# Splitting the first MLP into two blocks of two tiles, and replacing the two small ScalarE steps of the threshold search by one VectorE operation, in a hybrid-attention block

## The chip, the cores and the metric

The kernel runs on one core of a Trainium2 chip. The metric is device time in microseconds (us), the median of several runs; the parts are read from one execution taken by the hardware profiler.

## The reference

One transformer block in float32 on `x` of 1024 tokens by 1024 features. Three residual parts follow one another, each behind an RMS norm:

```
x = x + hybrid_mixer(rms_norm(x))      # DSA top-k attention, and NSA: compressed + window + selected
x = x + memory_xattn(rms_norm(x), mem) # 4 heads over 256 memory tokens
x = x + square(relu(rms_norm(x) @ w_ff_in)) @ w_ff_out   # 1024 -> 4096 -> 1024
...
idx_score = einsum(relu(q_i @ k_i), w_i)        # per query, over all earlier keys
_, sel = top_k(idx_score, 256)                  # DSA attends to those 256 keys alone
```

For this length the NSA branch selects every admissible block, so only DSA needs a search: for each query, the 256th largest index score.

## The kernel before

**Tiles and stages.** The 1024 tokens are eight tiles of 128, numbered 0 to 7. A head stage projects tiles 0 to 3. Then *attention* goes through tiles 0 to 7 (`attend`); beside it a second stream, the *fill*, does work that needs no attention yet or no longer: the projection of tiles 4 to 7, the memory's keys and values (`memory`), then for finished tiles `between` (output projection, norm, memory attention) and `mlp`. Behind attention come what is left of the fill, `between` for tiles 6 and 7, and the last MLP for tiles 4 to 7.

**Order.** `together` draws from two generators. Attention yields its estimated PE time; the fill is drawn while its own sum is at most `pace` times attention's. A tuple `(need, pace)` from the fill holds it until attention has passed tile `need` and sets a new pace; the paces are `PACES`. Behind attention, `merge` draws from the rest of the fill and from `between(d2, 6, 2, ...)` in proportion to `REST` and 45. The order of drawing is a priority; a scheduler of the framework then sets a fixed order of instructions for each engine, and each engine runs its list in order.

**The fill before.** `memory`, then `between(dn, 0, 2)`, `between(dn, 2, 2)`, `mlp(dn, 0, 4)` and `between(dn, 4, 2)`; the two numbers are the first tile and how many.

**MLP and weights.** A float32 product is made of three single-pass products of rounded parts (`whi`, `wlo` for weights; `xh`, `xl` or a pair of `h` tiles for data). `load_w` brings 256 KB into a `wraw` buffer, ScalarE rounds it into `whi` (L244), and the difference goes into `wlo` (L249), on GpSimd where the entry of `PLAN_MAIN` or `PLAN_TAIL` is "ag" and on VectorE where it is "av". Up-projection: stationary weights, moving data `[128, nt*128]`, 24 matmuls for each of 32 column groups. Down-projection: stationary data, 512 moving weight columns. The residual is added at L891. Where one pass is not needed in parts (`load_whole`, L265) a full float32 product is used; those weights share the buffers of `whi` and `wlo`.

**Rings.** `RINGS` gives the buffers of each tag in a pool. `dn` is the fill's pool, `d2` the last MLP's. PSUM has two banks of tag D and one of M for the fill, and S, PT, PV for attention; `d2` takes S and PT.

**The search.** `index_mask` for tile t+1 runs beside attention of tile t, for t+1 from 2 to 7: scores, then a binary search over 16 high and 16 low bits. Each step is three ScalarE operations, each waiting for the one before: count the scores over the threshold (`Sign` with `accum_out`, L636), compare the count (L637), move the threshold (L638).

Of the kernel before, what the change touches and what calls it, by code (L numbers as in the profile page):

```python
# [9 lines left out]
F32 = mybir.dt.float32  # L10
# [25 lines left out]
RINGS = {  # L36
    "p1": {"x4": 5, "st": 2, "relu": 4, "wraw": 4, "whi": 6, "wlo": 6, "c8": 4, "c4": 2, "kraw": 5, "pc": 2},
    "p2": {"x4": 3, "st": 1, "relu": 2, "whi": 4, "wlo": 4, "c8": 3, "c4": 1, "kraw": 4, "pc": 2},
    "dn": {"b4": 4, "h": 8, "relu": 2, "wraw": 2, "whi": 4, "wlo": 4},
    "d2": {"b4": 4, "h": 8, "relu": 2, "wraw": 3, "whi": 6, "wlo": 6},  # L40
}
PSUMS = {"p1": {"D": 4, "M": 3, "C": 1}, "main": {"S": 2, "PT": 2, "PV": 1, "D": 2, "M": 1}}
TAGS = {"p1": ("D", "M", "C"), "p2": ("D", "M", "D"), "dn": ("D", "M"), "d2": ("S", "PT")}
PLAN_HEAD = ("ag", "av")
PLAN_MAIN = ("ag",)
PLAN_TAIL = ("ag", "av", "ag")

SLC, WIN, DSA, IDX = 0, 2, 4, 5
# [28 lines left out]
        "c_cmask": np.ascontiguousarray(cm.transpose(1, 0, 2)),  # L77
    }
TC_ARGS = {"schedule_with_timeline_sim": True}
PACES = (1.35, 1.35, 1.35, 1.75, 1.75)  # L80
REST = 70.0


def drain(gen):
# [21 lines left out]
def merge(a, b):  # L106
    drain(beside(*a, *b))


def together(att, fill, projected):  # L110


    da = df = lead = 0.0
    tile_, need, part, pace = -1, -2, 0, PACES[0]
    la = lf = True
    while la:
        held = part > len(projected)
        if lead is None and need < tile_:
            lead = df - da * pace
        if lf and need < tile_ and (held or df <= lead + da * pace):  # L120
            w = next(fill, None)
            lf = w is not None
            if isinstance(w, tuple):
                need, pace = w
                lead = None
            else:
                df += w or 0.0
        else:
            assert not held
            x = next(att, None)  # L130
            la = x is not None
            if la and x[1] is None:
                part += 1
            elif la:
                tile_ = x[0]
                da += x[1]


# [28 lines left out]
def build(nc, tc, I, C, out):  # L167
# [92 lines left out]

    def load_whole(pool, shape, *srcs):
        wholes["i"] += 1
        raw = ring(pool, ("whi", "wlo")[wholes["i"] % 2], shape)
        for dst, src in srcs:
            nc.sync.dma_start(dst(raw), src)  # L265
        return [raw]
# [58 lines left out]
                consume(ci, t, pt)  # L325
                yield nk * (5 - len(xs)) * w / 2400.0

    def xT(pool, nt, whole=False):

        parts = [pool.tile([P, DM // P, nt * P], F32 if whole else F32R, tag="x" + n, name="x" + n)  # L330
                 for n in ("h" if whole else "hl")]
        return (parts, [lambda t, k, x=x: x[:, k, t * P:(t + 1) * P] for x in parts],
                lambda t: [x[:, :, t * P:(t + 1) * P] for x in parts])

# [257 lines left out]
    def index_mask(aw, st, t):  # L592
        Wd = (t + 1) * P
        acc = small(aw, "isc", L, bufs=1)
        for hg in range(2):
            qh, ql = q_prep(aw, t, 2, hg)
            for h in range(4):
                for c, n in chunks_of(t + 1):
                    sp = pst("S", [P, n * P])
                    mv = st["K"][:, IDX, c * P:(c + n) * P]  # L600
                    mm(sp, qh[:, h, :], mv, True, False)
                    mm(sp, ql[:, h, :], mv, False, True)
                    r = small(aw, "ir", 512)
# [12 lines left out]
        sgn = mask.bitcast(I16)  # L616
        hi, lo = small(aw, "tkh", L, U16, 1)[:, :Wd], small(aw, "tkl", L, U16, 1)[:, :Wd]
        v.tensor_scalar(sgn, bits[:, :, 1], 0.0, -1.0, op0=ALU.is_lt, op1=ALU.mult)
        v.scalar_tensor_tensor(hi.bitcast(I16), sgn, -32768, bits[:, :, 1], op0=ALU.bitwise_or, op1=ALU.bitwise_xor)
        v.tensor_tensor(lo.bitcast(I16), bits[:, :, 0], sgn, op=ALU.bitwise_xor)  # L620


        cnt, low = small(aw, "tkc", 1), small(aw, "tkf", 1)
        over, step, need = small(aw, "tko", 1), small(aw, "tks", 1), small(aw, "tkg", 2)
        th = small(aw, "tkt", 2)
        v.memset(need[:, 0:1], Wd - 2 * TOPK + 1.0)
        v.memset(th, 0.5 - 32768.0)
        for half, src in enumerate((hi, lo)):
            c, nd = th[:, half:half + 1], need[:, half:half + 1]
            if half == 1:  # L630
                v.tensor_scalar(low, th[:, 0:1], -1.0, None, op0=ALU.mult)
                v.tensor_scalar(mask, hi, low, None, op0=ALU.is_gt, op1=ALU.add, accum_out=cnt)
                v.tensor_scalar(nd, cnt, 2.0, Wd - 2 * TOPK + 1.0, op0=ALU.mult, op1=ALU.add)
                v.scalar_tensor_tensor(lo, hi, low, lo, op0=ALU.is_equal, op1=ALU.mult)
            for b in range(15, -1, -1):
                s.activation(mask, src, AF.Sign, bias=c, accum_out=over)  # L636
                s.activation(step, over, AF.Sign, bias=nd)  # L637
                s.activation(c, step, AF.Identity, scale=-0.5 * (1 << b), bias=c)  # L638
# [254 lines left out]

    def between(pool, t0, nt, x2s, keep):

        o_of = []
        for t in range(nt):
            o = ring(pool, "b4", [P, 8, P])
            for c in range(8):
                nc.sync.dma_start(o[:, c, :], oT_dr[t0 + t][c])  # L900
            o_of.append(o)
        x2 = [ring(pool, "b4", [P, DM]) for t in range(nt)]
        for t in range(nt):
            nc.sync.dma_start(x2[t], I["x"][0, (t0 + t) * P:(t0 + t + 1) * P, :])
        add_to = residual_add(x2)
        four = [[(c * 256, 256)] for c in range(4)]
        yield from gemm(pool, [lambda t, k: o_of[t][:, k, :]], 8, nt, W["w_out"], four, add_to)
        _, xf, xt_of = xT(pool, nt, True)

        gb2 = gain2(pool, W["norm2_g"])  # L910
        for t in range(nt):
# [82 lines left out]
    def mlp(pool, t0, nt, x2s):  # L994
# [13 lines left out]
        for f4 in range(8):  # L1008
# [24 lines left out]
            for c in range(2):  # L1033
# [4 lines left out]
                for t in range(nt):  # L1038
# [11 lines left out]
                                          x2[t][:, c * 512:(c + 1) * 512])  # L1050
                    yield 2.6

    def pe_stack():
        pe = p1.tile([P, 2, 32], F32, tag="pe", name="pe")
        pe2 = ring(p1, "relu", [P, 2, 2, 64])
# [18 lines left out]
        "dm": {},  # L1074
        "ix": set(),
    }
    for kv in range(2):
        v.memset(st["cT"][kv], 0.0)
    pe = pe_stack()
# [7 lines left out]
    dn_pool = tc.tile_pool(name="dn", bufs=1, reuse_waits="tile")  # L1087
    aw = aw_pool.__enter__()
    projected = []

    def fill():
        for part in range(1, len(PARTS)):
# [3 lines left out]
        dn = dn_pool.__enter__()  # L1096
        yield from memory(dn)
        yield 1, PACES[1]
        yield from between(dn, 0, 2, {}, False)
        yield 3, PACES[2]  # L1100
        x2s = {}
        yield from between(dn, 2, 2, x2s, True)
        yield 3, PACES[3]
        yield from mlp(dn, 0, 4, x2s)
        yield 5, PACES[4]
        yield from between(dn, 4, 2, {}, False)

    rest = fill()
    together(attend(aw, st), rest, projected)
    aw_pool.__exit__(None, None, None)  # L1110
    at_pool.__exit__(None, None, None)
    d2_pool = tc.tile_pool(name="d2", bufs=1, side="right", reuse_waits="tile")
# [1 line left out]
    d2 = d2_pool.__enter__()  # L1114
    x2s = {}
    rest = (w for w in rest if not isinstance(w, tuple))
    merge((rest, REST), (between(d2, 6, 2, x2s, True), 45.0))
    dn_pool.__exit__(None, None, None)
    drain(mlp(d2, 4, 4, x2s))
    d2_pool.__exit__(None, None, None)  # L1120
    ctx.close()

# [20 lines left out]
```

## Time and profile before

| | us |
|---|---|
| median of 3 runs | 1808.53 (1806.28 to 1810.84) |
| the profiled execution, its own time | 1807.76 |
| its span in the trace | 1806.0 |
| TensorE busy, as recorded | 1700.2 |
| ScalarE busy | 1061.9 |
| VectorE busy | 927.8 |
| GpSimd busy | 887.4 |

PE is TensorE's matmul row, PEld its weight loads, DVE is VectorE, ACT ScalarE, POOL GpSimd, SP the queue that issues DMAs. A matmul's record is longer than the time for which it holds the array, because matmuls overlap; the distance between the starts of two matmuls in a dense stretch tells what one costs. A row of a group reads: line, engine, operation, output<-inputs, shape, count | busy us, mean ns of one | idle time of the engine just before, and what ended it. A row of the table by stages gives the stretch, its length, and for each engine busy us and, in brackets, instructions; then the granted TensorE clock, the DMA share and GB/s.

### The profile page before, as it was taken

The numbers are of one execution on the slowest core, as the hardware profiler recorded it, in microseconds if no ns is written. First come the engines' busy times: TensorE is split into PE (matmuls) and PEld (weight loads), VectorE is DVE, ScalarE is ACT, GpSimd is POOL, SyncE is SP. The second block draws the span as 40 slices with busy tenths as digits, with TensorE's granted clock in tenths as the row PEclk, the third lists the DMA queues.
The fourth block names the chain that finished last, engine by engine and source line by source line (L and its number), as shares of the span: only waits on it lengthen the run. The fifth ranks groups of instructions, "written<-read, shape, count | busy, mean of one in ns | idle before, by whom it ended". The sixth has DMA issues, their size and how long they took to land. (4 is left out here: it accounts for less than half of the span.)

```text
span 1806.0 us, 27690 instructions
## 1 busy us (share of the span) xinstructions
PE 1700.2 (94%) x9134; PEld 1447.8 (80%) x9134; DVE 927.8 (51%) x2343; ACT 1061.9 (59%) x2655; POOL 887.4 (49%) x1015
## 2 busy tenths in 40 slices
PE   5987999899989999999998999999999799999998
PEld 5986888688878777788886888888888687787887
DVE  4545757665874776375754555646524322222221
ACT  4445669797688579855896558994513333333332
POOL 2356647363541355568575667662111144545444
PEclk9998999999999999999999999999999799999999
DMA  6235221366336211212122212226384122222222
GB/s 193 73 121 155 70 68 58 114 196 175 102 109 196 87 59 42 75 65 80 59 75 75 62 65 78 65 74 194 98 284 151 47 87 89 97 91 96 94 95 93
DMA packets 171887, 185.38 MB, mean 103 GB/s; under 512 B 26464, under 2 KB 140896, under 8 KB 171744
## 3 DMA queue, kind: packets, MB, share of 16 engines
q1 hardware_dynamic: 163808, 173.13, 30.3%
q0 software_dynamic: 7936, 10.49, 2.2%
q8 instruction: 72, 1.18, 0.3%
q14 instruction: 71, 0.58, 0.1%
HBM read 162.59 MB, written 20.97 MB: 102 GB/s over the span
## 5 line engine op out<-in xcount | busy, mean ns | idle before, releaser
L249 POOL TENSOR_TENSOR wlo<-wraw,whi 128x512 fp32r<-128x512 f32 (+1 forms) x231 | 310.6, 1351 | 280.9 <-ACT whi L244 252.9
L244 ACT ACTIVATE whi<-wraw 128x512 fp32r<-128x512 f32 (+2 forms) x289 | 181.0, 628 | 250.8 <-PE psS L218 156.8
L218 PE MATMUL psD<-whi,xh 128*128 128x256 f32 (+1 forms) x704 | 191.1, 352 | 4.4 <-ACT whi L244 3.4
L218 PE MATMUL psD<-wlo,xh 128*128 128x256 f32 (+1 forms) x704 | 190.3, 352 | 1.6 <-DMA wlo<-in_w_in_dram 1.0
L236 DVE TENSOR_TENSOR pl<-psPT,ph 128x512 fp32r<-128x512 f32 (+1 forms) x232 | 142.1, 621 | 78.9 <-ACT ph L235 76.3
L218 PE MATMUL psD<-whi,h 128*128 128x512 f32 x512 | 174.3, 403 | 3.7 <-ACT whi L244 1.6
L218 PE MATMUL psS<-whi,h 128*128 128x512 f32 x512 | 162.4, 392 | 5.4 <-DVE b L891 5.4
L680 ACT ACTIVATE S<-S,mn 128x128 f32<-128x128 f32 (+7 forms) x192 | 142.7, 744 | 40.5 <-DVE mn L678 39.0
L685 POOL TENSOR_SCALAR S<-S,sums,gi 128x640 f32<-128x640 f32 (+7 forms) x128 | 107.8, 853 | 114.1 <-DVE sums L683 103.5
L235 ACT ACTIVATE ph<-psPT 128x512 fp32r<-128x512 f32 (+1 forms) x232 | 122.9, 540 | 61.5 <-PE psPT L695 57.1
L249 DVE TENSOR_TENSOR wlo<-wraw,whi 128x512 fp32r<-128x512 f32 (+1 forms) x58 | 56.3, 971 | 170.3 <-ACT whi L244 170.1
L218 PEld LDWEIGHTS psD<-wlo,xh 128*128 128x128 f32 x704 | 132.4, 193 | 13.6 <-DMA wlo<-in_w_in_dram 1.4
L218 PEld LDWEIGHTS psD<-whi,xh 128*128 128x128 f32 x704 | 130.0, 193 | 14.2 <-ACT whi L244 3.8
L695 PE MATMUL psPT<-c_ident,S 128*128 128x128 f32 x816 | 131.8, 277 | 3.9 <-POOL S L685 2.6
L891 DVE TENSOR_TENSOR b<-psS,b 128x512 f32<-128x512 f32 (+1 forms) x80 | 49.9, 636 | 138.5 <-PE psS L218 138.5
L218 PE MATMUL psS<-K,qh 128*128 128x384 f32 (+3 forms) x288 | 112.4, 394 | 8.9 <-DVE mn L678 3.9
L218 PEld LDWEIGHTS psS<-whi,h 128*128 128x128 f32 x512 | 96.0, 188 | 30.4 <-DVE b L891 10.1
L218 PEld LDWEIGHTS psD<-whi,h 128*128 128x128 f32 x512 | 95.5, 189 | 25.8 <-ACT whi L244 2.0
L695 PEld LDWEIGHTS psPT<-c_ident,S 128*128 128x128 f32 x816 | 97.6, 142 | 14.1 <-POOL S L685 4.5
L218 PE MATMUL psD<-wlo,h 128*128 128x512 f32 x256 | 102.6, 404 | 1.1 <-POOL wlo L249 1.1
L218 PE MATMUL psD<-xh,wlo 128*128 128x512 f32 x256 | 101.5, 398 | 0.0
L891 DVE TENSOR_TENSOR b<-psD,b 128x512 f32<-128x512 f32 (+1 forms) x112 | 63.2, 573 | 74.0 <-PE psD L218 66.9
(289 smaller groups left out, 4546.2 us busy)
## 6 DMA issues: line engine op xcount, KB each, us to landing
wraw<-in_w_ff_in_dram SPq DMA_DIRECT2D x128, 256.0 KB, 2.7
wraw<-in_w_ff_out_dram SPq DMA_DIRECT2D x128, 256.0 KB, 2.6
whi<-in_w_out_dram SPq DMA_DIRECT2D x32, 256.0 KB, 3.8
wlo<-in_w_out_dram SPq DMA_DIRECT2D x32, 256.0 KB, 4.3
wraw<-in_w_in_dram SPq DMA_DIRECT2D x24, 256.0 KB, 3.4
q<-st SPq DMA_DIRECT2D x12, 512.0 KB, 2.6
qin<-q SPq DMA_DIRECT2D x44, 128.0 KB, 2.3
x<-in_x_dram SPq DMA_DIRECT2D x8, 512.0 KB, 5.5
```

The source lines that it names most:

```text
L218: te.matmul(o, a, b, start=start, stop=stop)
L235: s.activation(hi, src, AF.Copy)
L236: v.tensor_tensor(lo, src, hi, op=ALU.subtract)
L244: s.activation(hi, raw, AF.Copy)
L249: (v if l == "v" else g).tensor_tensor(lo, raw, hi, op=ALU.subtract)
L680: s.activation(S, S, AF.Exp, bias=low, scale=-1.0, accum_out=sums[:, hh:hh + 1])
L685: g.tensor_scalar(Ss[hh], Ss[hh], sums[:, hh:hh + 1], 1.0 if gate is None else gate[:, hh:hh + 1], op0=ALU.mult, op1=ALU.mult)
L695: te.transpose(p2[:, j, hh, :], S[:, (c + j) * P:(c + j + 1) * P], ident)
L891: v.tensor_tensor(dst, pt, dst, op=ALU.add)
```

## The change

Five edits belong together.

1. `mlp(dn, 0, 4)` becomes `mlp2` twice, for tiles 0 and 1 and for tiles 2 and 3. A block's up-projection moves 256 columns instead of 512, and each block loads and splits all MLP weights, so that they are loaded twice. `mlp2` has rings of its own (`hs`, `mr`).
2. The fill's order: `between(0, 2)`, then `two_streams`, which draws the MLP blocks as the main stream and, beside it, `between` for one tile at a time: tile 2, tile 3 (before the second block may start), then tiles 4 and 5 beside the second block. A single tile may start once attention has left it behind.
3. `load_whole` in pool `dn` has a ring of its own, `wb`, of two buffers, instead of the eight of `whi` and `wlo`.
4. In the search, the compare and the move become one VectorE `scalar_tensor_tensor` with accumulator: of three columns [-2^b, threshold, 2^b/2] those whose count exceeds the need are summed; two columns always do.
5. `PLAN_MAIN` sends a third of the `wlo` subtractions to VectorE, the last two paces go from 1.75 to 1.5, and behind attention `between(6, 2)` is followed by the first steps (the norms) of the last MLP, both beside the rest of the fill.

The diff, cut; `mlp2` is otherwise `mlp` with two tiles.

```diff
-    "dn": {"b4": 4, "h": 8, "relu": 2, "wraw": 2, "whi": 4, "wlo": 4},
+    "dn": {"b4": 4, "h": 7, "hs": 8, "mr": 2, "relu": 2, "wb": 2, "wraw": 2, "whi": 4, "wlo": 4},
-PLAN_MAIN = ("ag",)
+PLAN_MAIN = ("ag", "av", "ag")
-PACES = (1.35, 1.35, 1.35, 1.75, 1.75)
-REST = 70.0
+PACES = (1.35, 1.35, 1.35, 1.5, 1.5)
+SIDE = 0.9
+REST = 110.0
...
-        raw = ring(pool, ("whi", "wlo")[wholes["i"] % 2], shape)
+        raw = ring(pool, "wb" if "wb" in RINGS.get(pool.name, ()) else ("whi", "wlo")[wholes["i"] % 2], shape)
...
-        over, step, need = small(aw, "tko", 1), small(aw, "tks", 1), small(aw, "tkg", 2)
+        over, tks, need = st["tko"], st["tks"], small(aw, "tkg", 2)
         th = small(aw, "tkt", 2)
-        v.memset(need[:, 0:1], Wd - 2 * TOPK + 1.0)
-        v.memset(th, 0.5 - 32768.0)
+        v.memset(need[:, 0:1], 2.0 * TOPK - 1.0 - Wd)
         for half, src in enumerate((hi, lo)):
-            c, nd = th[:, half:half + 1], need[:, half:half + 1]
+            nd = need[:, half:half + 1]
             if half == 1:
                 v.tensor_scalar(low, th[:, 0:1], -1.0, None, op0=ALU.mult)
                 v.tensor_scalar(mask, hi, low, None, op0=ALU.is_gt, op1=ALU.add, accum_out=cnt)
-                v.tensor_scalar(nd, cnt, 2.0, Wd - 2 * TOPK + 1.0, op0=ALU.mult, op1=ALU.add)
+                v.tensor_scalar(nd, cnt, -2.0, 2.0 * TOPK - 1.0 - Wd, op0=ALU.mult, op1=ALU.add)
                 v.scalar_tensor_tensor(lo, hi, low, lo, op0=ALU.is_equal, op1=ALU.mult)
             for b in range(15, -1, -1):
-                s.activation(mask, src, AF.Sign, bias=c, accum_out=over)
-                s.activation(step, over, AF.Sign, bias=nd)
-                s.activation(c, step, AF.Identity, scale=-0.5 * (1 << b), bias=c)
+                i = 15 - b
+                s.activation(mask, src, AF.Sign, bias=tks[:, i, 1:2], accum_out=over[:, 0:1])
+                v.scalar_tensor_tensor(small(aw, "tkj", 3), over, nd, tks[:, i, :], op0=ALU.is_gt, op1=ALU.mult,
+                                       accum_out=tks[:, i + 1, 1:2] if b else th[:, half:half + 1])
                 yield 0.1
...
-        o_of = []
+        one = "b" if nt == 1 else "h"
+        (o,), xf, _ = xT(pool, nt, True, one)
         for t in range(nt):
-            o = ring(pool, "b4", [P, 8, P])
             for c in range(8):
-                nc.sync.dma_start(o[:, c, :], oT_dr[t0 + t][c])
-            o_of.append(o)
+                nc.sync.dma_start(o[:, c, t * P:(t + 1) * P], oT_dr[t0 + t][c])
         x2 = [ring(pool, "b4", [P, DM]) for t in range(nt)]
         for t in range(nt):
             nc.sync.dma_start(x2[t], I["x"][0, (t0 + t) * P:(t0 + t + 1) * P, :])
         add_to = residual_add(x2)
         four = [[(c * 256, 256)] for c in range(4)]
-        yield from gemm(pool, [lambda t, k: o_of[t][:, k, :]], 8, nt, W["w_out"], four, add_to)
-        _, xf, xt_of = xT(pool, nt, True)
+        yield from gemm(pool, xf, 8, nt, W["w_out"], four, add_to)
+        _, xf, xt_of = xT(pool, nt, True, one)
...
+    def mlp2(pool, t0, x2s):
...
+                c0 = (f4 * 4 + f2 * 2) * P
+                for k0 in range(0, 8, KG):
+                    hi, lo = load_w(pool, [P, KG, 256], (lambda r: r, W["w_ff_in"][k0 * P:(k0 + KG) * P, c0:c0 + 256]
+                                                         .rearrange("(k p) n -> p k n", p=P)))
...
+                    pt = pst(TAGS[pool.name][0], [P, 256])
+                    fs = slice(f * P, (f + 1) * P)
+                    for k in range(8):
+                        wh, wl = gr[k]
+                        mm(pt, wh[:, fs], xh[:, k, :], k == 0, False)
+                        mm(pt, wl[:, fs], xh[:, k, :], False, False)
+                        mm(pt, wh[:, fs], xl[:, k, :], False, k == 7)
+                    hh, hl = ring(pool, "hs", [P, 256], F32R), ring(pool, "hs", [P, 256], F32R)
+                    r = ring(pool, "mr", [P, 256])
+                    s.activation(r, pt, AF.Relu)
+                    s.activation(r, r, AF.Square)
+                    g.tensor_scalar(hh, r, 1.0, 1.0, op0=ALU.mult, op1=ALU.mult)
+                    g.tensor_tensor(hl, r, hh, op=ALU.subtract)
+                    hs.append((hh, hl))
+                    yield 2.6
...
+    st["tks"] = at.tile([P, 16, 3], F32, tag="tks", name="tks")
+    st["tko"] = at.tile([P, 3], F32, tag="tko", name="tko")
+    v.memset(st["tko"], BIG)
+    v.memset(st["tks"][:, 0, 1:2], 0.5 - 32768.0)
+    for i in range(16):
+        v.memset(st["tks"][:, i, 0:1], -1.0 * (1 << (15 - i)))
+        v.memset(st["tks"][:, i, 2:3], 0.5 * (1 << (15 - i)))
...
-        yield from between(dn, 0, 2, {}, False)
-        yield 3, PACES[2]
         x2s = {}
-        yield from between(dn, 2, 2, x2s, True)
-        yield 3, PACES[3]
-        yield from mlp(dn, 0, 4, x2s)
-        yield 5, PACES[4]
-        yield from between(dn, 4, 2, {}, False)
+        yield from between(dn, 0, 2, x2s, True)
+        yield seen["tile"] - 1, PACES[2]
+        yield from two_streams(dn, x2s)
+
+    def two_streams(dn, x2s):
+
+
+        main, mains = mlp2(dn, 0, x2s), 1
+        side, t = None, 2
+        dm = ds = 0.0
+        while main or side or mains < 2 or t < 6:
+            if side is None and t < 6 and seen["tile"] > t and (t < 4 or mains == 2):
+                side, ds = between(dn, t, 1, x2s, t < 4), dm
+                if t == 4:
+                    yield seen["tile"] - 1, PACES[3]
+            if main is None and mains == 1 and side is None and t >= 4:
+                main, mains = mlp2(dn, 2, x2s), 2
+            if side and (main is None or ds <= dm):
+                w = next(side, None)
+                ds += (w or 0.0) / SIDE
+                if w is None:
+                    side, t = None, t + 1
+            elif main:
+                w = next(main, None)
+                dm += w or 0.0
+                if w is None:
+                    main = None
+            elif t < 6:
+                w = t, PACES[3]
+            if w is not None:
+                yield w
 
     rest = fill()
-    together(attend(aw, st), rest, projected)
+    together(attend(aw, st), rest, projected, seen)
+    seen["tile"] = NT
     aw_pool.__exit__(None, None, None)
     at_pool.__exit__(None, None, None)
     d2_pool = tc.tile_pool(name="d2", bufs=1, side="right", reuse_waits="tile")
@@ -1114,9 +1203,10 @@
     d2 = d2_pool.__enter__()
     x2s = {}
     rest = (w for w in rest if not isinstance(w, tuple))
-    merge((rest, REST), (between(d2, 6, 2, x2s, True), 45.0))
+    last = mlp(d2, 4, 4, x2s)
+    merge((rest, REST), (chain(between(d2, 6, 2, x2s, True), take(last, 4.0)), 62.0))
     dn_pool.__exit__(None, None, None)
-    drain(mlp(d2, 4, 4, x2s))
+    drain(last)
     d2_pool.__exit__(None, None, None)
```

More of the change, by code (lines that the diff above doesn't have):

```diff
@@ L107, in merge, with together @@
     drain(beside(*a, *b))
-def together(att, fill, projected):
+def together(att, fill, projected, seen):
     da = df = lead = 0.0
@@ L134, in together @@
             elif la:
-                tile_ = x[0]
+                tile_ = seen["tile"] = x[0]
                 da += x[1]
@@ L326, in gemm, with xT @@
                 yield nk * (5 - len(xs)) * w / 2400.0
-    def xT(pool, nt, whole=False):
+    def xT(pool, nt, whole=False, one="h"):
         parts = [pool.tile([P, DM // P, nt * P], F32 if whole else F32R, tag="x" + n, name="x" + n)
-                 for n in ("h" if whole else "hl")]
+                 for n in (one if whole else "hl")]
         return (parts, [lambda t, k, x=x: x[:, k, t * P:(t + 1) * P] for x in parts],
@@ L1051, in mlp @@
                     yield 2.6
+    def mlp2(pool, t0, x2s):
+        x2 = [x2s[t0], x2s[t0 + 1]]
+        (xh, xl), _, xt_of = xT(pool, 2)
+        gb3 = gain2(pool, W["norm3_g"])
+        for t in range(2):
+            norm_T2(pool, x2[t], gb3, xt_of(t))
+            yield 1.0
+        for f4 in range(8):
+            hs = []
+            for f2 in range(2):
+                gr = []
+                c0 = (f4 * 4 + f2 * 2) * P
+                for k0 in range(0, 8, KG):
+                    hi, lo = load_w(pool, [P, KG, 256], (lambda r: r, W["w_ff_in"][k0 * P:(k0 + KG) * P, c0:c0 + 256]
+                                                         .rearrange("(k p) n -> p k n", p=P)))
+                    gr += [(hi[:, k, :], lo[:, k, :]) for k in range(KG)]
+                for f in range(2):
+                    pt = pst(TAGS[pool.name][0], [P, 256])
[13 more added lines that the diff above has]
+                    yield 2.6
+            for c in range(2):
+                cs = slice(c * 512, (c + 1) * 512)
+                gr = []
+                for k in range(4):
+                    r0 = (f4 * 4 + k) * P
+                    gr.append(load_w(pool, [P, 512], (lambda r: r, W["w_ff_out"][r0:r0 + P, cs])))
+                for t in range(2):
+                    pt = pst(TAGS[pool.name][0], [P, 512])
+                    us = slice(t * P, (t + 1) * P)
+                    for f in range(4):
+                        hh, hl = hs[f]
+                        wh, wl = gr[f]
+                        mm(pt, hh[:, us], wh, f == 0, False)
+                        mm(pt, hh[:, us], wl, False, False)
+                        mm(pt, hl[:, us], wh, False, f == 3)
+                    v.tensor_tensor(x2[t][:, cs], pt, x2[t][:, cs], op=ALU.add)
+                    if f4 == 7:
+                        nc.sync.dma_start(out[0, (t0 + t) * P:(t0 + t + 1) * P, cs], x2[t][:, cs])
+                    yield 2.6
@@ L1089, in build @@
     projected = []
+    seen = {"tile": -1}
     def fill():
```

## The prediction

> **What bounds the kernel now.** I read the page first, then the table by stages, then single stretches of the timeline, to learn what a matmul costs where nothing holds it.
>
> ```profile
> PE 1700.2 (94%) x9134; PEld 1447.8 (80%) x9134; DVE 927.8 (51%) x2343; ACT 1061.9 (59%) x2655; POOL 887.4 (49%) x1015
> ```
>
> TensorE looks 94% busy, but its records overlap. The timeline shows the true price by the distance of starts:
>
> ```profile
> 100.11 0.28 PE L218 MATMUL psD<-whi,xh 128*128 128x256 f32 x1
> ...
> 100.45 0.28 PE L218 MATMUL psD<-whi,xh 128*128 128x256 f32 x1
> ...
> 103.74 0.82 PE L474 MATMUL psM<-c_ident,x 128*128 128x128 f32 x6
> 104.31 0.37 PE L218 MATMUL psD<-whi,xl 128*128 128x256 f32 x1
> ```
>
> ```profile
> 1417.15 1.03 PE L218 MATMUL psS<-wlo,xh 128*128 128x256 f32 x4
> 1418.02 1.03 PE L218 MATMUL psS<-whi,xh 128*128 128x256 f32 x4
> ...
> 1500.08 0.39 PE L218 MATMUL psS<-xh,whi 128*128 128x512 f32 x1
> 1500.31 0.40 PE L218 MATMUL psS<-xh,wlo 128*128 128x512 f32 x1
> ```
>
> A single-pass matmul costs 0.23 us for 512 columns and 0.113 for 256 (the two rows quoted are three matmuls apart: 0.34/3). A record of a full float32 product with 256 columns costs 0.87/4 = 0.216, and each such product has two. Six transposes take 0.57 us; I round up to 0.11 each. Weighing all 9134 records so (other widths in proportion, nothing below 0.11) gives 1,599 us of unavoidable TensorE work. The span is 1806.0, so 207 us are lost. The stages:
>
> ```profile
> 0.00:145.00 145.00, 110.63 (x910) 107.98 (x910) 69.50 (x159) 64.82 (x174) 55.37 (x62) 0.96 0.43 131
> 145.00:210.00 65.00, 60.56 (x351) 52.80 (x351) 43.69 (x166) 40.28 (x142) 43.77 (x80) 0.95 0.42 121
> 210.00:300.00 90.00, 89.37 (x527) 79.07 (x528) 60.12 (x211) 63.96 (x233) 52.17 (x82) 1.00 0.21 57
> 300.00:411.00 111.00, 98.65 (x521) 83.47 (x520) 78.81 (x222) 95.31 (x297) 59.78 (x87) 0.94 0.45 142
> 411.00:538.00 127.00, 118.59 (x701) 103.23 (x700) 87.90 (x246) 95.80 (x270) 57.21 (x87) 0.99 0.44 130
> 538.00:713.00 175.00, 165.19 (x939) 141.17 (x938) 116.37 (x335) 135.39 (x348) 71.27 (x91) 0.98 0.31 98
> 713.00:926.00 213.00, 209.25 (x1085) 175.05 (x1083) 121.07 (x268) 156.45 (x357) 144.40 (x145) 1.00 0.22 71
> 926.00:1150.00 224.00, 218.32 (x1122) 181.76 (x1121) 124.86 (x279) 158.31 (x346) 148.23 (x146) 0.98 0.22 68
> 1150.00:1304.00 154.00, 151.75 (x859) 131.72 (x857) 92.27 (x230) 100.70 (x222) 63.09 (x66) 0.99 0.36 114
> 1304.00:1440.00 136.00, 121.14 (x600) 103.88 (x598) 50.10 (x129) 37.20 (x86) 19.00 (x28) 0.88 0.53 165
> 1440.00:1806.00 366.00, 356.75 (x1538) 287.68 (x1536) 83.09 (x106) 113.64 (x187) 173.08 (x146) 1.00 0.28 92
> ```
>
> From 210 on, the cuts are the ends of attention tiles 1 to 7. Length less weighed work is the loss: 39 us in the head, 17 in tiles 0 and 1, then tile by tile (2 to 7) 32, 17, 27, 10, 13, 8, then 33 from 1304 to 1440, and 11 in the last MLP. So the kernel is bound by TensorE's work, and a change can gain only in the 207. Two places hold half of it: tiles 2 to 4 (76), where ScalarE is busy 327 of 413 us, and the stretch behind attention (33), where every engine is often idle. Its end reads:
>
> ```profile
> 1409.43 1.09 PE L274 MATMUL psPT<-c_ident,relu 128*128 128x128 f32 x4 [3.60 <-DMA relu<-xo]
> ...
> 1429.79 1.30 PE L274 MATMUL psPT<-c_ident,relu 128*128 128x128 f32 x8 [2.98 <-DVE relu L297]
> ```
>
> TensorE waits there for one chain after another, having no other work, and the granted clock of the stage is 0.88.
>
> **The change part by part.** *TensorE's work.* The first MLP's up-projection had 32 x 24 = 768 matmuls of 512 columns, 177 us; it gets 1536 of 256, 174 us. All other products keep their number. I book -3.
>
> *Where the fill stands.* The two programs' order on TensorE, weighed alike, gives the fill between the first value products of one tile and the next: before 52, 66, 96, 142, 147, 85 us for tiles 2 to 7 and 31 behind attention; after 42, 58, 74, 87, 100, 64 and 190. So 160 us of work move behind attention; attention must become shorter by as much, or time is lost. Tiles 5 to 7 then hold 182 us of attention and 252 of fill, 434 in place of 555.
>
> *Behind attention* (1304 to 1440), the second MLP block now stands among both chains, and the last MLP's norms before the block's end, so the waits quoted above are covered. Of 33 us I leave 13, near the 11 of the last stage that also has MLP matmuls throughout: -20 (bounds -25 and 0: the wait for `xo` can still end last).
>
> *The search.*
>
> ```profile
> L638 ACT ACTIVATE tkt<-tks,tkt 128x1 f32<-128x1 f32 x192 | 55.8, 291 | 3.0
> L637 ACT ACTIVATE tks<-tko,tkg 128x1 f32<-128x1 f32 x192 | 55.5, 289 | 2.3
> ...
> L678 DVE DVE_READ_ACCUMULATOR2_ANT mn<- 128x1 f32 x256 | 20.8, 81 | 0.0
> ...
> L743 DVE TENSOR_SCALAR csum<-csum 128x2 f32<-128x2 f32 x32 | 9.5, 297 | 9.8 <-ACT cS L741 9.5
> ```
>
> ```profile
> 300.00:538.00 238.00, 16.84 (x58) 0.96 0.44 135
> 538.00:713.00 175.00, 10.18 (x35) 0.98 0.31 98
> ```
>
> 192 steps lose 0.29 + 0.29 us of ScalarE, 111 us in all; the second fence (L637 alone by stages) places 93 of them in tiles 2 to 4, which is 54 us. VectorE gains 192 operations that the trace doesn't show: between an accumulator read alone (0.081) and a small operation with one (0.297 + 0.081), 16 to 73 us; I take 0.30, nearest to the small operation. The step now crosses to VectorE and back, and its next `Sign`, with all that ScalarE has queued behind it (`whi`, `ph`, the exponentials), waits for VectorE's turn. If every step stands behind one `pl` subtraction,
>
> ```profile
> L236 DVE TENSOR_TENSOR pl<-psPT,ph 128x512 fp32r<-128x512 f32 x176 | 119.6, 686 | 63.5 <-ACT ph L235 61.2 <-PE psD L218 1.4
> ```
>
> a step grows by 0.30 + 0.69 - 0.58 = 0.4 us, 38 us over the 93. So the effect lies between -54 and +38 us; since ScalarE is 79% busy there and VectorE 69%, I take -30, a little over half of what is freed.
>
> *Thinner fill in tiles 5 to 7.* Their loss was 31 of 591 us, 5%. With 1.4 us of fill for each us of attention instead of 2.1 they come to resemble tile 4 (1.8 and 15%). Between 5 and 15% I take 11% of 434, 49 us: +18 (bounds -9 and +34).
>
> *The `wb` ring.*
>
> ```profile
> whi<-in_w_out_dram SPq DMA_DIRECT2D x32, 256.0 KB, 3.8
> wlo<-in_w_out_dram SPq DMA_DIRECT2D x32, 256.0 KB, 4.3
> ...
> whi<-in_w_xo_dram SPq DMA_DIRECT2D x16, 256.0 KB, 3.0
> ```
>
> 176 loads go through two buffers instead of eight. By the new order, 34 of them have less than 3.0 us of TensorE work between the release of the buffer and the first use of what comes into it. At a landing of 3.0 us they lack 27 us together, half of that since two buffers share a wait; at 4.3 the lack is about 60. I take +10, near the low end, as these products lie in stretches that lose time anyway. Behind a `wb` load that waits on SP stand `wraw` loads, `qin` loads and stores of `oc`. SP also gets some 190 more issues, covered by a queue that has them early.
>
> *Weights twice.*
>
> ```profile
> L249 POOL TENSOR_TENSOR wlo<-wraw,whi 128x512 fp32r<-128x512 f32 x228 | 307.0, 1353 | 280.8 <-ACT whi L244 252.9 <-DMA wraw<-in_w_ff_in_dram 23.9 <-PE psS L218 2.2
> L244 ACT ACTIVATE whi<-wraw 128x512 fp32r<-128x512 f32 x284 | 178.5, 630 | 250.7 <-PE psS L218 156.8 <-DMA wraw<-in_w_ff_in_dram 49.1 <-PE psD L218 13.2
> ...
> L249 DVE TENSOR_TENSOR wlo<-wraw,whi 128x512 fp32r<-128x512 f32 x56 | 55.1, 984 | 169.8 <-ACT whi L244 169.6
> ```
>
> 128 more `whi` cost ScalarE 81 us; the order has 42 more `wlo` on GpSimd (57 us) and 86 more on VectorE (85 us). More than half of them lie behind attention, where ScalarE is busy 37 of 136 us; inside it they replace those of the work that moved out. I book nothing; without that cover they are the first rival.
>
> Whether VectorE's subtractions hold up GpSimd's, the trace can say, since the last MLP already shares them and the first doesn't:
>
> ```profile
> 713.00:1150.00 437.00, 0.00 (x0) 142.69 (x105) 0.99 0.22 70
> 1440.00:1800.00 360.00, 39.81 (x40) 108.48 (x82) 1.00 0.28 92
> ```
>
> GpSimd takes 142.69/105 = 1.36 us for one beside none of VectorE's, 1.32 beside 40: no lengthening. The Trainium skill says otherwise ("SBUF — State Buffer", section "Who interferes with whom"): a VectorE instruction with two SBUF inputs and a GpSimd instruction that reads SBUF exclude each other for a whole instruction. By it, GpSimd would lose up to 86 x 0.98 = 84 us; the trace disagrees.
>
> *The sum*, from the profiled execution's 1807.8 (its span 1806.0 and 1.8 around it; the median of the runs, 1808.53, is 0.8 above): -3 - 20 - 30 + 18 + 10 = -25, so 1783.
>
> **The rivals.** *The weights' way becomes the bound.* A block's 128 loads stand beside 175 us of its matmuls, 1.4 us each, where the four-tile block gave 2.8. In tile 6 the order has 100 us of the block, so 73 loads in 167 us: 2.3 us each.
>
> ```profile
> wraw<-in_w_ff_in_dram SPq DMA_DIRECT2D x128, 256.0 KB, 2.7
> ```
>
> ```profile
> SPq L254 <- POOL wlo L249: 606.8, 207, 18.7
> ```
>
> One load through a ring of two takes (2.7 + 0.63 + 1.23)/2 = 2.3 us, with nothing in the way (1.23 mixes 1.35 and 0.98 two to one). It ties exactly. Behind attention's operations on ScalarE and GpSimd, 0.6 us each, it becomes 2.9: 212 us for tile 6 where I have 167 + 18, +27; with tile 7 and the start behind attention some +45, so 1828. It decides from about 2.5 us a load. For it speaks that loads stood 607 us for GpSimd's release of the buffer; against it, that ScalarE and GpSimd lose attention's small steps and a third of `wlo`. Chance 0.24.
>
> *ScalarE was the bound in tiles 2 to 4*: the whole 54 us come out and thin fill costs nothing: 1807.8 - 3 - 20 - 54 + 0 + 0 = 1731. Chance 0.14.
>
> *The search gains nothing*, because VectorE's turn takes as long as the two steps did: 1783 + 30 = 1813. Chance 0.12.
>
> *The shared port counts after all.* If each added VectorE subtraction held GpSimd for its 0.98 us, tile 6 alone would lose 24 of them; about 20 us in all would reach the end: 1803. The quoted 1.36 against 1.32 leaves 0.03. This is the rule quoted above from the Trainium skill, "SBUF — State Buffer".
>
> **How the numbers follow.** The forecast, 1783, has 0.47; its own range is 1760 to 1805. Over all cases 1735 to 1835 leaves out most of the second rival's far side and the first one's worst. About 0.3% (5.4 us) is what a measurement of this kernel can tell from no change. Faster by more: 0.44 of the forecast, 0.14 and 0.01, so 0.59. Within: 0.03, 0.07, 0.02 and 0.01, so 0.13. Slower: 0.23 and 0.05, so 0.28.
>
> **What would show it.** Right: attention ends about 150 to 190 us earlier (near 1130), the loss in tiles 2 to 4 falls to about 46, and no wait of 3 us is left before the last MLP. The new VectorE operation has a mean near 0.3 us. Wrong: `psD<-whi,xh` or `psD<-wlo,hs` waiting for `whi` and `wlo` by tens of us in tiles 5 to 7 (first rival), matmuls waiting for `wb` by more than 30, or ScalarE idle behind the new operation.

## The result, and the profile after

The changed kernel takes 1909.99 us (median; 1907.63 to 1916.12) against 1808.43: 1.0566 times as long, 95% interval 1.0538 to 1.0595. That is 102 us slower, where the prediction had 25 us faster and ended its range at 1835.

The page of the changed kernel, its totals, two groups of line 250 (the `wlo` subtraction, L249 before) and one of line 245 (`whi`, L244 before):

```profile
span 1905.7 us, 30130 instructions
...
PE 1734.2 (91%) x9902; PEld 1495.3 (78%) x9902; DVE 1039.7 (55%) x2841; ACT 1050.6 (55%) x2463; POOL 968.1 (51%) x1137
...
L250 POOL TENSOR_TENSOR wlo<-wraw,whi 128x512 fp32r<-128x512 f32 (+2 forms) x273 | 364.3, 1341 | 363.9 <-ACT whi L245 345.7
L245 ACT ACTIVATE whi<-wraw 128x512 fp32r<-128x512 f32 x417 | 258.1, 628 | 386.9 <-PE psS L219 132.4
L250 DVE TENSOR_TENSOR wlo<-wraw,whi 128x512 fp32r<-128x512 f32 x144 | 134.0, 931 | 280.0 <-ACT whi L245 279.6
```

No engine became a bound by its total: TensorE's share of busy time fell from 94 to 91%. The table by stages (length, then busy us and instructions of PE, PEld, DVE, ACT and POOL, granted clock, DMA share, GB/s), cut at the ends of attention tiles 1 to 7 and where the second MLP block is over:

```profile
210.00:303.00 93.00, 92.40 (x543) 82.23 (x541) 67.67 (x268) 63.33 (x220) 50.81 (x81) 1.00 0.23 65
303.00:399.00 96.00, 85.20 (x464) 72.18 (x463) 77.31 (x242) 74.50 (x207) 57.50 (x80) 0.95 0.39 130
399.00:531.00 132.00, 116.23 (x637) 97.82 (x636) 89.95 (x294) 84.12 (x217) 61.10 (x92) 0.94 0.38 110
531.00:698.00 167.00, 142.39 (x863) 123.72 (x861) 121.67 (x396) 115.21 (x273) 71.60 (x96) 0.96 0.37 114
698.00:879.00 181.00, 164.17 (x982) 142.38 (x982) 129.49 (x365) 125.92 (x276) 98.45 (x118) 0.97 0.45 139
879.00:1084.00 205.00, 190.45 (x1201) 165.61 (x1200) 145.82 (x368) 154.15 (x331) 142.94 (x157) 0.98 0.34 107
1084.00:1227.00 143.00, 131.91 (x837) 115.34 (x835) 108.47 (x267) 99.16 (x203) 71.44 (x77) 0.99 0.43 134
1227.00:1550.00 323.00, 296.90 (x1588) 255.28 (x1589) 97.27 (x187) 113.89 (x229) 136.62 (x142) 0.97 0.55 177
1550.00:1905.00 355.00, 343.17 (x1542) 279.62 (x1540) 88.10 (x107) 115.61 (x198) 178.27 (x158) 0.99 0.32 104
```

Weighed with the spacings of the prediction, TensorE's work is 1,597 us against 1,599: the same. The loss went from 207 to 309 us. By tile, 2 to 7, with the loss before in brackets: 28 (32), 30 (17), 42 (27), 35 (10), 34 (13), 22 (8); behind attention 62 (44), and the rest as before. So attention ended at 1227 and not at 1304, 77 us earlier, but it should have become shorter by the 160 us of work that left it.

The chain of work that ended last, followed back from the last instruction, now holds landings of `wraw` for some 5% of the span (the two rows of 3 and 2%) and the subtraction on GpSimd for 3%:

```profile
PE psS L219 22%; PE psD L219 19%; POOL wlo L250 3%; DMA wraw<-in_w_ff_in_dram 3%; PE psPV L219 2%; DMA wraw<-in_w_ff_out_dram 2%; PE psPT L698 2%; ACT dmask L639 2%; DMA wb<-in_w_xq_dram 2%; ACT whi L245 1%; DMA wb<-in_w_out_dram 1%; ACT S L683 1%; DVE S L681 1%; POOL S L688 1%; DVE pl L237 1%
```

What the rounding of the weights waits for, from the waits of ScalarE, after:

```profile
ACT whi L245 <- DMA wraw<-in_w_ff_out_dram: 97.9, 63, 9.4
ACT whi L245 <- DMA wraw<-in_w_ff_in_dram: 97.0, 63, 4.6
```

and before:

```profile
ACT whi L244 <- DMA wraw<-in_w_ff_in_dram: 49.1, 26, 4.2
...
ACT whi L244 <- DMA wraw<-in_w_ff_out_dram: 10.5, 13, 2.0
```

ScalarE stood 195 us for a load to land (60 before), and in tile 6 the rounding and the subtraction (lines 245 and 250 alone, as a table by stages) read:

```profile
879.00:1084.00 205.00, 45.11 (x72) 0.98 0.34 107
```

```profile
879.00:1084.00 205.00, 21.39 (x24) 65.04 (x48) 0.98 0.34 107
```

72 loads in 205 us, 2.85 us each. The first rival had put 73 loads at 2.9 us, 212 us for this tile; the forecast had 185. The length alone doesn't tell the cause: a_no_split below has 203 us for the tile without these loads. Nor do TensorE's own waits, of which the largest for weights are

```profile
PE psD L219 <- ACT whi L245: 13.2, 12, 3.8
...
PE psD L219 <- DMA wb<-in_w_xq_dram: 9.3, 7, 3.1
PE psD L219 <- DMA wb<-in_w_xo_dram: 9.0, 8, 3.3
```

Together they are 18 us for `whi` and `wlo` (6 before) and 26 for `wb` in the whole run, so the signs that the prediction named, tens of us in tiles 5 to 7 and more than 30, did not appear. The price shows where loads are left out.

### The profile page after: what moved, and what is told of

Its sections match the earlier page's. It is cut to its first block, busy times and chain, and to the rows that moved or that the text cites. A ratio compares the mean times of both kernels' runs of the same rounds, so it can differ in the third digit from the quotient of the medians.

```text
span 1905.7 us, 30130 instructions
## 1 busy us (share of the span) xinstructions
PE 1734.2 (91%) x9902; PEld 1495.3 (78%) x9902; DVE 1039.7 (55%) x2841; ACT 1050.6 (55%) x2463; POOL 968.1 (51%) x1137
## 4 chain that ended last, share of the span: by engine, by line
PE 47%; DMA 12%; DVE 8%; ACT 7%; POOL 6%; issue 4%; SPq 1%; ACTq 0%; POOLq 0%; DVEq 0%
PE psS L219 22%; PE psD L219 19%; POOL wlo L250 3%; DMA wraw<-in_w_ff_in_dram 3%; PE psPV L219 2%; DMA wraw<-in_w_ff_out_dram 2%; PE psPT L698 2%; ACT dmask L639 2%; DMA wb<-in_w_xq_dram 2%; ACT whi L245 1%; DMA wb<-in_w_out_dram 1%; ACT S L683 1%; DVE S L681 1%; POOL S L688 1%; DVE pl L237 1%
## 5 line engine op out<-in xcount | busy, mean ns | idle before, releaser
L250 POOL TENSOR_TENSOR wlo<-wraw,whi 128x512 fp32r<-128x512 f32 (+2 forms) x273 | 364.3, 1341 | 363.9 <-ACT whi L245 345.7
L245 ACT ACTIVATE whi<-wraw 128x512 fp32r<-128x512 f32 x417 | 258.1, 628 | 386.9 <-PE psS L219 132.4
L250 DVE TENSOR_TENSOR wlo<-wraw,whi 128x512 fp32r<-128x512 f32 x144 | 134.0, 931 | 280.0 <-ACT whi L245 279.6
L219 PE MATMUL psD<-whi,hs 128*128 128x512 f32 x512 | 179.7, 412 | 9.3 <-ACT whi L245 4.4
L219 PE MATMUL psD<-xh,whi 128*128 128x256 f32 x512 | 147.1, 297 | 7.4 <-ACT whi L245 5.0
L219 PE MATMUL psD<-wb,xb 128*128 128x256 f32 x512 | 133.0, 390 | 18.6 <-DMA wb<-in_w_xq_dram 7.9
L219 PE MATMUL psD<-xh,wlo 128*128 128x256 f32 x512 | 147.4, 292 | 1.1 <-POOL wlo L250 0.9
L219 PE MATMUL psD<-xl,whi 128*128 128x256 f32 x512 | 144.6, 286 | 0.0
L219 PEld LDWEIGHTS psD<-whi,hs 128*128 128x128 f32 x512 | 97.4, 193 | 33.7 <-ACT whi L245 5.9
L219 PEld LDWEIGHTS psD<-wb,xb 128*128 128x128 f32 x512 | 92.8, 193 | 35.5 <-DMA wb<-in_w_xq_dram 10.0
```

Source lines behind the costliest of these rows:

```text
L219: te.matmul(o, a, b, start=start, stop=stop)
L245: s.activation(hi, raw, AF.Copy)
L250: (v if l == "v" else g).tensor_tensor(lo, raw, hi, op=ALU.subtract)
```

## The experiments

Medians in us; the ratio is to the kernel before, with its interval. The runs that leave loads out do not compute the block; of them the time alone is read. The expectations go by theories: A, the two `wb` buffers cost the time; B, the search's way over VectorE holds up ScalarE's queue and with it attention; C, behind the thinner fill attention's own waits are bare; D, the way of the first MLP's weights is the bound, by the landing in two `wraw` buffers (D1) or by the splits (D2).

| run | median | ratio |
|---|---|---|
| changed kernel | 1910 | 1.0566 (1.0538 to 1.0595) |
| b_search | 1827 | 1.0106 (1.0079 to 1.0134) |
| b_two_buffers | 1871 | 1.0342 (1.0321 to 1.0362) |
| b_blocks | 1950 | 1.0779 (1.0747 to 1.0810) |
| b_blocks_search | 1973 | 1.0902 (1.0878 to 1.0926) |
| b_third_on_vector | 1826 | 1.0087 (1.0068 to 1.0106) |
| b_norms_beside | 1812 | 1.0004 (0.9995 to 1.0014) |
| a_old_search | 1931 | 1.0675 (1.0651 to 1.0698) |
| a_pairs | 1989 | 1.0988 (1.0965 to 1.1010) |
| a_gpsimd_alone | 1935 | 1.0681 (1.0659 to 1.0703) |
| a_three_wb | 1899 | 1.0483 (1.0464 to 1.0503) |
| a_no_reload | 1890 | 1.0454 (1.0437 to 1.0471) |
| a_no_landing | 1868 | 1.0322 (1.0302 to 1.0342) |
| a_no_split | 1841 | 1.0175 (1.0153 to 1.0197) |
| a_no_loads | 1804 | 0.9966 (0.9954 to 0.9977) |

Names with b start from the kernel before, names with a from the changed one.

**What the weights cost the changed kernel.** First the loads into `wb` alone, kept at the first two.

```diff
+        kept = wholes.setdefault(pool.name, [])
+        if "wb" in RINGS.get(pool.name, ()) and len(kept) == 2:
+            return [kept[wholes["i"] % 2]]
...
+        kept.append(raw)
```

> The changed kernel with the loads into wb left out, all but the first two: the full float32 products in the fill's pool all use the same two blocks of weights, so no matmul waits for one. Theory A: 1845 to 1860, as 50 to 60 us of waits on wb go. Theory B: 1895 to 1910. Theory C: 1880 to 1900, since the waits on wb fall together with attention's.

1890: 20 us, not the 50 to 60 of theory A; it lies in the range of theory C. Then the first MLP's weights, loaded and split for the first four loads alone.

```diff
+        if "wb" in RINGS.get(pool.name, ()):
+            i = wholes["j"] = wholes.get("j", -1) + 1
+            if i >= 4:
+                return [... for x in pairs[i % 4]]
```

> The changed kernel with the first MLP's weights loaded and split for the first four loads alone, and the other 252 loads of the two blocks left out; their matmuls use those four. It shows what the weights' way (load, whi, wlo) costs. Theory D (this way is the bound, as the first rival had it): 1840 to 1860. Theory C: 1880 to 1900, since attention's waits stay bare.

1841, 69 us less: in the range of theory D, and far below that of C. Both together:

> As the run before, and the loads into wb left out as well, so that no matmul of the fill behind the projections waits for a weight. Theory A and D together: 1790 to 1810. Theory C: 1860 to 1880; what is left is attention with too little beside it.

1804, so 106 us go. That is as much as the whole excess over the kernel before, and theory C's 1860 to 1880 is refuted. Two things limit this: with the loads the order of instructions changes too, and no run left the loads out of the kernel before, so how much of its own 207 us goes to weights is open. How it works shows tile 6 of a_no_split beside the changed kernel's row above (the same columns):

```profile
881.00:1084.00 203.00, 202.38 (x1321) 183.78 (x1320) 124.40 (x342) 116.32 (x251) 79.43 (x113) 1.00 0.12 39
```

The tile is no shorter, but 1321 matmuls stand in it in place of 1201, and TensorE is busy 202 of 203 us. What the fill can't do beside attention, because its weights aren't there, is left for afterwards: a_no_loads needs 587 us behind attention, with 19 us without a matmul's record,

```profile
1214.00:1801.00 587.00, 567.68 (x2768) 475.44 (x2766) 142.21 (x227) 160.22 (x293) 207.70 (x204) 0.99 0.28 92
```

the changed kernel 678, with 38.

```profile
1227.00:1905.00 678.00, 640.07 (x3128) 534.89 (x3128) 185.37 (x294) 229.49 (x426) 314.89 (x299) 0.98 0.43 139
```

Weighed, that is 557 us of work in place of 616. The kernel before had 458 there, so some 99 us of the 160 that moved behind attention stay there with every weight at hand; the weights are not why those moved.

**Landing or splitting.** Only the loads are left out, all splits made from the first two buffers.

```diff
+            if i < 2:
+                raws.append(ring(pool, "wraw", [P, 512]))
...
+            raw = raws[i % 2] if len(shape) == 2 else ...
```

> The changed kernel with the first MLP's weights loaded for the first two loads alone; all 256 splits into whi and wlo are still made, from those two buffers. With no split at all the kernel came to 1841, with everything to 1910. Theory D1 (the load's landing and the two wraw buffers are what holds a weight up): 1840 to 1855. Theory D2 (the splits' time on ScalarE, GpSimd and VectorE holds it up): 1890 to 1910.

1868, between the ranges of the two theories: 42 of the 69 us go with the loads and their two buffers, 27 with the splits. No run gave `wraw` a third buffer, so the landing and the number of buffers are not told apart. The subtraction on GpSimd alone:

```diff
-PLAN_MAIN = ("ag", "av", "ag")
+PLAN_MAIN = ("ag",)
```

> The changed kernel with every wlo of the fill's pool inside attention on GpSimd again, as before. Theory D1: 1905 to 1925, since the landing stays and a subtraction takes 0.4 us more than on VectorE. Theory D2: 1930 to 1960, since GpSimd gets 57 more of 1.34 us and attention's own behind them. If the shared port counted (last rival): below 1905.

1935, 25 us more: in the range of D2 and 10 us above that of D1. The last rival, the shared port, asked for less than 1905; taking subtractions off VectorE made the kernel slower, so whatever is shared costs less than what VectorE's third saves. It does not show that nothing is shared. In the tile 6 rows above GpSimd takes 65.04/48 = 1.36 us beside 24 subtractions on VectorE, as it did beside none, but in the trace only two of those 24 overlap one of GpSimd's, for 1.8 us in all. Where they do meet, one waits for the other; the rows stand in the last section. A third buffer for `wb`:

```diff
-    "dn": {"b4": 4, "h": 7, "hs": 8, "mr": 2, "relu": 2, "wb": 2, ...
+    "dn": {"b4": 4, "h": 6, "hs": 8, "mr": 2, "relu": 2, "wb": 3, ...
```

> The changed kernel with three wb buffers instead of two (and six of h instead of seven, for room). Leaving the wb loads out gave 20 us. Theory A: 1895 to 1902. If the bytes in flight don't matter and only the landing does: 1905 to 1910.

1899, in the range of theory A and about half of what no load at all gives.

**The parts put into the kernel before.** The two blocks, with the rings that they need and `between` bringing in its data as in the changed kernel:

```diff
-        yield from mlp(dn, 0, 4, x2s)
+        yield from mlp2(dn, 0, x2s)
+        yield from mlp2(dn, 2, x2s)
```

> The kernel before with the first MLP in two blocks of two tiles, one behind the other, and nothing else of the change (eight buffers for the full products, tiles by pairs, the search on ScalarE, the old paces). By its order on TensorE the fill in tiles 5 to 7 is 264 us instead of 374, and 146 us stand behind attention instead of 31. Theory A (the two wb buffers cost the time): 1800 to 1820. Theory C (behind the thinner fill attention's own waits are bare, and the blocks are what makes it thin): 1860 to 1890.

1950: more than either theory, and more than the whole change. Its TensorE waits point to the weights:

```profile
PE psD L218 <- POOL wlo L249: 31.3, 52, 2.2
PE psD L218 <- ACT whi L244: 17.2, 22, 3.4
```

Before, the same two rows were 1.1 and 5.0 us. These 49 us are a part of the 140; the rest is not traced to a cause. Two buffers for the full products' weights:

```diff
-        raw = ring(pool, ("whi", "wlo")[wholes["i"] % 2], shape)
+        raw = ring(pool, "wraw" if pool.name == "dn" else ("whi", "wlo")[wholes["i"] % 2], shape)
```

> The kernel before, but the weights of the full float32 products in the fill's pool go through two buffers (those of wraw) instead of the eight of whi and wlo. Theory A: 1835 to 1860; it has 112 loads of this kind where the changed kernel has 160, each beside twice the TensorE work. Theories B and C: within 10 us of 1808, since other work stands beside the waits.

1871, 62 us for 112 loads (the changed kernel has 176 of this kind, not the 160 of the expectation): above the range of theory A, and B and C are refuted for this part. Here other work beside the waits did not hide them. Its TensorE waits have

```profile
PE psD L218 <- DMA wraw<-in_w_out_dram: 23.6, 16, 5.1
```

The two streams, taken out of the changed kernel:

```diff
-        yield from two_streams(dn, x2s)
+        yield from between(dn, 2, 2, x2s, True)
...
+        yield from mlp2(dn, 0, x2s)
+        yield from mlp2(dn, 2, x2s)
+        yield 5, PACES[4]
+        yield from between(dn, 4, 2, {}, False)
```

> The changed kernel without its two streams: tiles 2 and 3, and 4 and 5, go through between as pairs, the two MLP blocks stand one behind the other in between. 64 fewer loads into wb. Theory A: 1885 to 1895, as a third of the wb loads goes. Theory C: 1900 to 1915, as the fill beside attention is as thin as with single tiles (262 us in tiles 5 to 7 by its order, 252 in the changed kernel).

1989, a miss for both: the streams are worth 79 us to the two blocks. That a block which waits for weights needs `between` beside it, and that the streams give it that, would fit; no run shows it.

**The search.** Alone in the kernel before, undone in the changed one, and with the two blocks alone; the edit is the search part of the diff each time.

> The kernel before with one part of the change alone: the search's compare and move as one VectorE operation. Theory A (the two wb buffers cost the time): this part is not the cause; it comes out at 1770 to 1810. Theory B (the step's way over VectorE holds up ScalarE's queue and with it attention): slower than before, 1830 to 1860. Theory C (behind the thinner fill attention's own waits are bare): as A, and below 1800, since the loss in tiles 2 to 4 falls.

> The changed kernel with the search's small steps back on ScalarE. Theory A: 1910 to 1940, since ScalarE gets 111 us back. Theory B: 1860 to 1885, as the crossing is gone. Theory C: 1915 to 1950, as attention has little fill to hide ScalarE's work behind.

> The kernel before with the two MLP blocks (1950 alone) and the search's one VectorE operation, nothing else of the change. If the blocks' 128 more whi make ScalarE short, so that the 111 us freed there count: 1920 to 1935. If the sign comes from something else of the change (wb, streams, VectorE's third): 1950 to 1970, as in the kernel before.

1827 (+18, outside every theory's range), 1931 (so the search saves 21 there, as A and C had it) and 1973 (+23 on b_blocks). The new operation, its line in the changed kernel (min/median/max ns), and its group with the mean:

```profile
L640 DVE SCALAR_TENSOR_TENSOR tkj<-tko,tkg,tks x192: 190/222/1281, 258.3 to 1136.9; 128x3 f32<-128x3 f32 x192
L640 DVE DVE_READ_ACCUMULATOR tkj<-tko,tkg,tks x192: 70/81/89, 258.5 to 1137.1; 128x1 f32 x192
...
  ACT dmask L639: 52.2, 73
who waited for it (us, times):
  ACT dmask L639: 19.2, 40
```

```profile
L640 DVE SCALAR_TENSOR_TENSOR tkj<-tko,tkg,tks 128x3 f32<-128x3 f32 x192 | 60.7, 316 | 53.5 <-ACT dmask L639 52.2
...
L640 DVE DVE_READ_ACCUMULATOR tkj<-tko,tkg,tks 128x1 f32 x192 | 15.4, 80 | 0.0
```

With the read of its accumulator it costs 0.30 us by the median, as forecast, but 0.40 by the mean: 76 us in all, just above the 73 that the prediction had as the most. ScalarE waits only 19 us for it (27 in b_search), so theory B's blockade is not seen. Yet in tiles 2 to 4 of b_search ScalarE fell from 327 to 274 busy us, and time was still lost:

```profile
304.00:402.00 98.00, 89.70 (x489) 76.89 (x488) 79.36 (x257) 76.05 (x216) 55.28 (x80) 0.95 0.42 136
402.00:531.00 129.00, 119.19 (x687) 101.86 (x685) 96.01 (x304) 83.65 (x221) 61.95 (x95) 0.97 0.44 127
531.00:707.00 176.00, 159.47 (x893) 138.60 (x894) 122.94 (x411) 114.56 (x270) 62.73 (x84) 0.94 0.33 103
```

The weighed work of these three is 318 us, so 85 us are lost, not fewer than the 76 before. So ScalarE, though busy, was not what held these tiles up; what did is not shown. Why the sign turns in the changed kernel is open: the last of the three runs refutes the doubled `whi` as its cause.

**Two pieces that might beat the kernel before.**

```diff
-PLAN_MAIN = ("ag",)
+PLAN_MAIN = ("ag", "av", "ag")
```

> The kernel before with a third of the wlo subtractions of the first MLP on VectorE. If GpSimd's subtraction holds weights up there too: 1790 to 1803. If the four-tile block gives each weight time enough (2.8 us of TensorE work): 1804 to 1812.

```diff
-    merge((rest, REST), (between(d2, 6, 2, x2s, True), 45.0))
+    last = mlp(d2, 4, 4, x2s)
+    merge((rest, REST), (chain(between(d2, 6, 2, x2s, True), take(last, 4.0)), 49.0))
```

> The kernel before with one piece of the change: the last MLP's norms are drawn behind between(6, 2) and beside the rest of the fill, not after both. The wait ahead of the last MLP has 33 us of loss in its stage. If the order of drawing decides: 1790 to 1800. If the chains' own waits decide, since the norms of tiles 6 and 7 need their results: 1803 to 1810.

1826 and 1812. The third on VectorE costs 16 us where a weight has 2.8 us of work (a miss; why is not shown), and the norms drawn beside the rest change nothing. None of the runs that compute the whole block is faster than the kernel before.

## Why the prediction was wrong, point by point

- *TensorE's work, -3*: right. The loss alone changed.
- *Weights twice, "I book nothing"*: the step that failed first. It measured 69 us: 42 go with the loads and their two buffers, 27 with the splits. The cover that was named, an idle ScalarE behind attention, was there, but ScalarE's busy time was not the main price: with every split still made, the 42 go. The price is a chain of load, rounding and subtraction through two buffers, 2.3 us by the prediction's own rows with nothing in the way, beside 1.4 us of matmuls that a weight now feeds in a block of two tiles (12 of 256 columns at 0.113 us). The first rival described it, and was given 0.24 and 45 us.
- *The `wb` ring, +10*: 20 us by itself, 37 once the other weights are out of the way. The bounds, 0 to 60, held; the value was taken near the low end because "these products lie in stretches that lose time anyway", and b_two_buffers with 62 us shows that such waits add up.
- *The search, -30*: -21 in the changed kernel, +18 in the kernel before. The bounds, -54 to +38, held, and so did the sign in the changed kernel, but the reason given did not: tiles 2 to 4 lost 76 us with ScalarE 79% busy, the prediction took the busy engine for the one that ends last, and in b_search, with ScalarE 52 us less busy there, they lost 85. The sign in the changed kernel is therefore luck as far as the runs show.
- *Thinner fill, +18* (11% of 434 is 48, not 49, so by its own working +17): the loss in tiles 5 to 7 went from 31 to 91. That the fill is thin was read rightly from the order. With every weight at hand (a_no_loads, weighed alike) the loss there is about 39, within the term's bounds, so the term failed by what it left to the weights.
- *Behind attention, -20*: 62 in place of 44. With all loads out it is 30 (587 us less 557 of work), so the cover works nearly as described when the covering block has its weights.
- *The shared port* (0.03): "no lengthening" and "the trace disagrees" were misread. The prediction compared GpSimd's means, and the subtraction that is held up is mostly VectorE's: in its own second row VectorE's 40 take 39.81/40 = 1.00 us, where one alone takes 0.69. Two subtractions that meet do exclude each other, in the kernel before as in the changed one (last section). Its size is small: taken as their time above 0.69 us, VectorE's 144 subtractions lost 35 us to instructions of GpSimd in the changed kernel, and its 58 lost 16 before. How much of that reaches the end no run shows; a_gpsimd_alone bounds it only against VectorE's gain.

With the two weight terms at their measured size (69 and 37 in place of 0 and 10) and nothing for the search, the prediction's own sum gives 1783 + 69 + 27 + 30 = 1909. That it meets 1910 is luck: the terms overlap, and with the search at -21 or +18 the sum is 1888 or 1927.

## What to carry to other kernels

Ask of each loaded block how much matmul time it feeds, and compare it with the time of its way through its buffers (load, conversion, hand-overs, over the number of buffers). Halving the work per load at an unchanged ring can turn a covered transfer into one that is paid, though every engine's busy share looks harmless and TensorE's work is the same. Leaving the loads out prices them better than TensorE's waits do: 106 us here, where the waits for weights add up to 44. And a mean over a group can hide that some of its instructions are held up.

## What the runs showed of the hardware that was not expected

That a subtraction on VectorE and one on GpSimd, both with two inputs in SBUF (the on-chip memory), run one after the other where they meet. In the kernel before, alone, where GpSimd is in one, and where GpSimd starts during one:

```profile
1473.41 0.69 DVE L249 TENSOR_TENSOR wlo<-wraw,whi 128x512 fp32r<-128x512 f32 x1 [0.65 <-ACT whi L244]
```

```profile
1552.59 1.31 POOL L249 TENSOR_TENSOR wlo<-wraw,whi 128x512 fp32r<-128x512 f32 x1
1552.80 1.65 DVE L249 TENSOR_TENSOR wlo<-wraw,whi 128x512 fp32r<-128x512 f32 x1 [8.56 <-ACT whi L244]
```

```profile
1460.93 1.75 DVE L249 TENSOR_TENSOR wlo<-wraw,whi 128x512 fp32r<-128x512 f32 x1 [8.92 <-ACT whi L244]
1462.36 1.50 POOL L249 TENSOR_TENSOR wlo<-wraw,whi 128x512 fp32r<-128x512 f32 x1 [0.23 <-ACT whi L244]
```

VectorE's takes 0.69 us alone; begun inside GpSimd's, it ends 0.55 us after that one's end (1554.45 against 1553.90). Of the 44 that began so in the changed kernel, 42 ended 0.55 us after, at 1.27 us in the mean. GpSimd's, begun inside VectorE's, ends 1.18 us after it (1463.86 against 1462.68), where alone it takes 1.31.

That a landing becomes no slower and is yet paid. In b_two_buffers 112 loads that had gone through the buffers of `whi` and `wlo` go through the two of `wraw`, and the kernel is 62 us slower, though these loads land sooner than before: the row of its DMA issues that covers 48 of them has 2.6 us, where the same 48 of the kernel before (its DMA issues up to 1304 us) have 3.5.

```profile
wraw<-in_w_out_dram SPq DMA_DIRECT2D x48, 256.0 KB, 2.6
```

```profile
whi<-in_w_out_dram SPq DMA_DIRECT2D x24, 256.0 KB, 3.5
wlo<-in_w_out_dram SPq DMA_DIRECT2D x24, 256.0 KB, 3.5
```

The median from issue to landing says what one load takes, not how many must be under way.
